# Seventy-two instead of sixty-seven seven-product pairs in the down projections of a two-layer encoder

## The chip, the core and the metric

The kernel runs on one core of one Trainium2 chip. A core has a matmul engine (TensorE, PE in the profile; its loading of stationary operands is PEld), an engine for element-wise work (VectorE, DVE), one that applies functions and copies (ScalarE, ACT), GpSimd (POOL) and SyncE (SP). Each issues its instructions in the order in which they were laid down and waits where an operand is not there yet. SP, ACT and POOL also issue transfers between the chip's memory and the core's. The metric is the device time of the whole kernel in microseconds, median over runs.

## The reference

Two encoder layers over one sequence of 256 tokens, width 2048, in float32. Each layer has an attention part with 12 heads of its own kind and 4 heads into 256 memory tokens, an output projection, and an MLP with a squared ReLU:

```
for i in range(2):
    h = rms_norm(x, norm_attn[i])
    ... heads = concat(token mixer's 12 heads, 4 memory heads)
    x = x + heads @ w_out[i]                        # 2048 x 2048
    h = rms_norm(x, norm_mlp[i])
    x = x + square(relu(h @ w_up[i])) @ w_down[i]   # 2048 x 8192, 8192 x 2048
```

Layer 0 has differential attention (two softmaxes subtracted), layer 1 windowed attention with a sink logit per head. The change bears on `@ w_down[i]`, the down projection of each layer, and on the first microseconds of the kernel.

## The kernel before

**Tiling.** Every weight matrix is cut into pieces of 128 x 1024 values (512 KB) and read once, in the order of one long list, the plan: input projection, memory projection, out, up and down of layer 0, then the same of layer 1. `fetch` takes the next piece from the plan: SP loads it into a raw tile (a `raw` buffer), and `split` makes two rounded halves of it, `hi` by a cast on ACT (line 443) and `lo`, the rest, by a subtraction on DVE (line 444). A product of float32 blocks is then three matmuls of 128x512 (x·hi, x·lo, and x's rest·hi), which `three` issues (lines 535 to 537; 496 to 498 in the input projection). `piece` keeps the fetched pieces two ahead of the matmuls.

**Down.** A down projection has two halves of the output columns, and each half goes through 32 k pairs. A k pair is two pieces. A **plain** pair takes eight products, 24 matmuls. A pair in the table of fast pairs takes **seven** products, 21 matmuls, with Winograd's scheme (function `seven`): it multiplies four sums of weight blocks (the tiles `a` and `b`, each 128x1024) and three differences of activation blocks (tile `t2`). For that DVE makes `b` in two additions of 128x512 (lines 357 and 358, in `sum_pair`), and `a` and `b` are each split into hi and lo: two casts more on ACT, two subtractions more on DVE. Tile `a` itself, piece one plus the upper part of piece two, was summed long before by transfers of POOL's queue into the chip's memory (`make_sums`, tensor `madesum`: a copy, then a transfer that adds), so that SP only loads it (line 339). These premade sums are spread over the plan by the steps in `SUM_GAP`. The differences of activations are made in the first half of down or in up, stored to memory (`kept`) and loaded by POOL for the half that uses them.

**Buffers.** The first piece of a fast pair, its `a` and its `b` lie in `slots`, a ring of six 128x1024 tiles (all named `big` in the profile). `load_pair` loads pairs up to three ahead (`LOOK`), as soon as a slot is free: the tile `a` of one fast pair goes into a slot that an earlier fast pair's first piece gives back when DVE has split it. The second piece's lower part goes into a 2 KB buffer (`t2k`). The split sums lie in tiles of the tags x2 or blk; in the second half of layer 0 the list `LATE_BLK` says which pair takes blk. They are returned when PE has used them.

**The order.** The program's text fixes the order on every engine: a scheduler lays each engine's instructions down once, and the wait queues are first in, first out. The tables `FAST` and `LATE` say which of the 32 pairs are fast. `FAST` (17 pairs) is used by both halves of layer 1 and the first half of layer 0, `LATE` (16) by the second half of layer 0:

```
WARM = 10
FAST = (2, 4, 6, 7, 9, 11, 12, 14, 16, 17, 19, 21, 22, 24, 26, 27, 29)
LATE = (2, 4, 6, 9, 11, 12, 14, 16, 17, 19, 21, 22, 24, 26, 27, 29)
LATE_BLK = (9, 12, 16, 19, 22, 26, 29)
```

**The start.** Ten matmuls of 128x128 on a tile `ones`, filled by DVE, run while the first transfers are under way (`WARM`, line 139). All x tiles and the first weight piece are loaded by SP. A tile `rw` holds a row of scalars, positions and sink logits, loaded once.

Of the kernel before, what the change touches and what calls it, by code (L numbers as in the profile page):

```python
# [14 lines left out]
F32 = mybir.dt.float32  # L15
F32R = mybir.dt.float32r
BF16 = mybir.dt.bfloat16
I32 = mybir.dt.int32
# [4 lines left out]
P = 128  # L23
S = 256
# [21 lines left out]
SQ_WAIT = 3  # L46
SINGLE = 4
AHEAD = 2
WARM = 10
FAST = (2, 4, 6, 7, 9, 11, 12, 14, 16, 17, 19, 21, 22, 24, 26, 27, 29)  # L50
LATE = (2, 4, 6, 9, 11, 12, 14, 16, 17, 19, 21, 22, 24, 26, 27, 29)
AWAY = range(6, 15)
LATE_BLK = (9, 12, 16, 19, 22, 26, 29)
LOOK = 3
KEEP_AFTER = (2, 6, 10, 14)
KEEP_LAST = (10, 18, 26, 34)
KEEP_GAP = 2
SUM_AT = {0: 44, 1: 2}
SUM_GAP = ({"in": 4, "mem": 4, "out": 4, "up": 11}, {"in": 4, "mem": 12, "out": 12, "up": 7})
LAM_INIT = 0.8 - 0.6 * math.exp(-0.3 * 0)  # L60

G_ATTN, G_MEM, G_MLP = 0, 2 * KT, 4 * KT
G_AQ, G_AK, G_BQ, G_BK = 96, 97, 98, 99
G_MQ, G_MK, G_SUB = 100, 102, 104
NG = 105
R_SINK = 256
R_POS = 268
NR = 524


@with_exitstack
def trunk(ctx: ExitStack, tc: tile.TileContext, xin, xtok, memin, memtok, posrel, gcol, rows,
          w_a, w_b, w_mem, w_out, w_up, w_down, out):
    nc = tc.nc

    cp = ctx.enter_context(tc.tile_pool(name="cp", bufs=1))
    wp = ctx.enter_context(tc.tile_pool(name="wp", bufs=4))
    xp = ctx.enter_context(tc.tile_pool(name="xp", bufs=1))
    tp = ctx.enter_context(tc.tile_pool(name="tp", bufs=1))
# [5 lines left out]
    def nm(s):  # L85
        uid[0] += 1
        return f"{s}{uid[0]}"

    def bank(tag="aux"):
        return pp.tile([P, 512], F32, tag=tag, name=nm(tag))  # L90
# [22 lines left out]
    def big(shape):  # L113
        return xp.tile(shape, F32, tag="big", name=nm("big"), bufs=1)

    def t2k(shape, dt=F32):
        return tp.tile(shape, dt, tag="t2k", name=nm("t2k"), bufs=7)

    def t1k():
        return tp.tile([P, 256], F32, tag="t1k", name=nm("t1k"), bufs=4)  # L120

    def small(n):
        return tp.tile([P, n], F32, tag="sm", name=nm("sm"), bufs=25)
# [4 lines left out]

    gc = cp.tile([P, NG], F32, name="gc")
    nc.scalar.dma_start(gc[:, 0:KT], gcol[:, 0:KT])  # L130
    xt = cp.tile([P, 2, D], F32, name="xt")
    nc.scalar.preload_act_table_set("natural_log_exp_and_others")
    ident = cp.tile([P, P], F32, name="ident")
    make_identity(nc, ident)
    ones = cp.tile([P, P], F32, name="ones")
    nc.vector.memset(ones, 1.0)
    warm = bank()
    for _ in range(WARM):
        nc.tensor.matmul(warm[:, 0:P], lhsT=ones, rhs=ones, start=True, stop=True)
    r2 = cp.tile([P, 2], F32, name="r2")  # L140
    ssq = cp.tile([P, 2, 4], F32, name="ssq")
    gs = cp.tile([P, 5], F32, name="gs")
    neglam = cp.tile([P, 1], F32, name="neglam")
    rw = cp.tile([P, NR], F32, name="rw")

    def inv_sqrt(dst, src, n):
        y = small(n)
# [92 lines left out]
    def fast_pairs(name, h):  # L240

        if name.startswith("out"):
            return OUT_FAST[h]
        if name.startswith("up"):
            return UP_FAST[h]
        if name.startswith("down"):
            return LATE if (name, h) == ("down0", 1) else FAST
        return ()

    def plan_pairs(name, n, halves=2):  # L250
# [25 lines left out]
    def sums_tag(key):  # L276
        if key[0].startswith("up"):
            return "h2"
        if key[0] == "down0" and key[1] == 1:
            return "blk" if key[2] in LATE_BLK else "x2"  # L280
        return "blk" if key[0].startswith("out") else "x2"
# [4 lines left out]
    def make_sums(layer):  # L286
# [15 lines left out]
        def step(i):  # L302
            if i:
                add(*wanted[i - 1])
            if i < len(wanted):
                copy(*wanted[i])
# [4 lines left out]
        for i in range(len(wanted) + 1):  # L311
            making.append((at, lambda i=i: step(i)))
            at += SUM_GAP[layer][max((k for k in SUM_GAP[layer] if at_piece[k, layer] <= at), key=lambda k: at_piece[k, layer])]

# [313 lines left out]
    def val_split(ps, st):  # L628
        hi = blk([P, 2, 512], F32R)
        lo = blk([P, 2, 512], F32R)  # L630
        for t in range(2):
            split_gain(hi[:, t, :], lo[:, t, :], ps[t], st[:, 2 + t:3 + t])
        return hi, lo
# [146 lines left out]
    tabs = {}  # L780

    def bias_distance():
        pr = cp.tile([P, 50], F32, name="posrel")
        with tc.issue_after(behind[0].ins):
            nc.sync.dma_start(pr, posrel)
        tabs["pr"] = pr
        pk, pq = pr[:, 0:2].bitcast(I32), rw[:, R_POS:R_POS + S].bitcast(I32)
        tabs["d"] = t2k([P, 2, S], I32)
        for t in range(2):
            nc.gpsimd.tensor_tensor(tabs["d"][:, t, :], pk[:, t:t + 1].broadcast_to([P, S]), pq, op=ALU.subtract)  # L790
# [70 lines left out]

    def load_rows():
        with tc.issue_after(behind[0].ins):
            nc.sync.dma_start(rw, rows.broadcast_to([P, NR]))
            nc.sync.dma_start(gc[:, KT:NG], gcol[:, KT:NG])

    def scalars():
        lv = rw[:, 0:256].rearrange("p (a b d) -> p a b d", a=2, b=2)
        pr = t1k()[:, 0:128].rearrange("p (a d) -> p a d", a=2)
        nc.vector.tensor_tensor(pr, lv[:, :, 0, :], lv[:, :, 1, :], op=ALU.mult)  # L870
        lm = small(2)
        nc.vector.tensor_reduce(lm, pr, axis=AX.X, op=ALU.add)
        le = small(2)
        nc.scalar.activation(le, lm, AF.Exp)
        nc.vector.tensor_tensor(neglam, le[:, 1:2], le[:, 0:1], op=ALU.subtract)
        nc.vector.tensor_scalar_add(neglam, neglam, -LAM_INIT)
        nc.vector.tensor_scalar_mul(gs[:, 0:1], gc[:, G_AQ:G_AQ + 1], 64 ** -0.5)
        nc.vector.tensor_scalar_mul(gs[:, 1:2], gc[:, G_BQ:G_BQ + 1], 128 ** -0.5)
        nc.vector.tensor_scalar_mul(gs[:, 2:4], gc[:, G_MQ:G_MQ + 2], 128 ** -0.5)
        nc.vector.tensor_scalar_mul(gs[:, 4:5], gc[:, G_SUB:G_SUB + 1], 1.0 - LAM_INIT)  # L880
# [64 lines left out]
    done_heads = {}  # L945
# [230 lines left out]
    X2 = Halves()  # L1176
    st0 = cp.tile([P, 4], F32, name="st0")

    xs = {}

    def load_x(k, n):
        if k % 4 == 0:
            xs[k // 4] = xp.tile([P, 4, S], F32, tag="h2", name=nm("xs"), bufs=6)
        nc.sync.dma_start(xs[k // 4][:, k % 4:k % 4 + n, :], xin[:, S * k:S * (k + n)].rearrange("p (k s) -> p k s", s=S))
# [13 lines left out]
    bias = big([P, 12, 2, S])  # L1198
# [5 lines left out]
    H2 = Halves(lambda pair: "h2" if pair < 6 else "x2")  # L1204
    make_sums(0)
    loads = Task([lambda c=c: load_residual(c) for c in range(4)], wait=RES_AT, gap=RES_GAP, front=True)
    for g in range(3):
# [18 lines left out]
        qT, qd = norm_T(ps, st0, 8, gs[:, 0:1])  # L1226
        ps = chunk_tok("a", 3 + g, X2)
        kT, kd = norm_T(ps, st0, 8, gc[:, G_AK:G_AK + 1])
# [3 lines left out]
    qm, qd = norm_T(ps, st0, 4, gs[:, 2:3])  # L1232
# [6 lines left out]
    H2 = Halves(lambda pair: "h2" if pair < 6 else "x2")  # L1239
    bias = bias_load()  # L1240
# [3 lines left out]
    kT, kd = norm_T(ps, st1, 4, gc[:, G_BK:G_BK + 1])  # L1244
    ps = chunk_tok("b", 4, X2)
    vv = val_split(ps, st1)
    for g in range(3):
        ps = chunk_tok("b", g, X2)
        qT, qd = norm_T(ps, st1, 4, gs[:, 1:2])
        for h in range(4):  # L1250
            n = 4 * g + h
            done_heads[n] = Task(plain_head(h, n // 3, qT, kT, vv, bias, rw[:, R_SINK + n:R_SINK + n + 1], H2, n), [qd, kd])
    ps = chunk_tok("b", 5, X2, mem_ahead)
    qm, qd = norm_T(ps, st1, 4, gs[:, 3:4])
    mem_part(1, qm, qd, H2)
# [71 lines left out]
```

## Time and profile before

| what | value |
|---|---|
| runs | 2071.48, 2071.71, 2073.93 us; median 2071.71 |
| profiled execution | 2070.87 us; its span 2069.1 us |
| matmuls busy (PE) | 2063.2 us, 9987 records |
| DVE, ACT, POOL busy | 1792.3, 1283.8, 179.9 us |
| down of layer 0, first half | 767 to 930 us |
| down of layer 0, second half | 930 to 1092 us |
| down of layer 1, first half | 1744 to 1906 us |
| down of layer 1, second half | 1906 to 2066 us |

The profile is of one execution, 0.84 us below the median of the runs. Busy time of PE counts pipelined matmuls whose ends are modelled: a 128x512 matmul is shown with 0.39 us although the next one starts 0.23 us later, so a matmul's cost is the distance of starts. The same holds, less strongly, for DVE and ACT. The rows by which the prediction argues stand there.

### The profile page before, as it was taken

What the parts mean: (1) busy time and instruction counts of PE and PEld (TensorE: products, weight loads), DVE (VectorE), ACT (ScalarE), POOL (GpSimd) and SP (SyncE); (2) the same over time, 40 slices, a digit from 0 to 9 for tenths busy, and PEclk for the clock granted to TensorE, in tenths of its full rate; (3) what the DMA queues carried; (4) which work ended last, traced back from release to release, by engine and by line L of the source; (5) the groups of instructions that cost most, each with busy time, mean ns of one, the idle gap of its engine ahead of it and who ended that gap; (6) DMA issues with size and microseconds to landing.
All of it is one profiled execution on the core that took longest, in us unless ns stands there. A gap on an engine that the chain in (4) does not pass through costs nothing.

```text
span 2069.1 us, 28771 instructions
## 1 busy us (share of the span) xinstructions
PE 2063.2 (100%) x9987; PEld 1715.1 (83%) x9987; DVE 1792.3 (87%) x2595; ACT 1283.8 (62%) x1912; POOL 179.9 (9%) x276
## 2 busy tenths in 40 slices
PE   9999999999999999999999999999999999999999
PEld 7888888888888888888888888888888888888887
DVE  7677777898998999998896677889998999999998
ACT  7467665556555577667665566556566566666764
POOL 1200111100010000000001110000001110000000
PEclk9999999999999999999999999999999999999999
DMA  9678997877888889988979887568889998998994
GB/s 316 243 241 271 278 289 226 275 231 224 267 283 280 289 280 337 363 290 281 343 277 298 270 261 214 193 217 253 255 269 315 307 300 301 341 356 309 299 361 167
DMA packets 172418, 577.80 MB, mean 279 GB/s; under 512 B 19936, under 2 KB 20960, under 8 KB 170976
## 3 DMA queue, kind: packets, MB, share of 16 engines
q1 hardware_dynamic: 133408, 441.19, 59.8%
q0 software_dynamic: 33824, 116.93, 22.0%
q10 hardware_dynamic: 5040, 17.84, 2.1%
q8 instruction: 78, 1.28, 0.2%
q14 instruction: 68, 0.56, 0.1%
HBM read 543.25 MB, written 100.79 MB: 311 GB/s over the span
## 4 chain that ended last, share of the span: by engine, by line
PE 97%; DVE 2%; DMA 1%; issue 0%; ACT 0%; SPq 0%; ACTq 0%; DVEq 0%
PE mm L536 12%; PE mm L537 12%; PE mm L535 12%; PE aux L536 11%; PE aux L537 11%; PE aux L535 11%; PE mm L496 7%; PE mm L497 7%; PE mm L498 7%; DVE lo L444 1%; PE aux L639 1%; PE mm L1043 1%; PE aux L1043 1%; PE aux L616 1%; PE aux L658 1%; PE aux L696 1%
## 5 line engine op out<-in xcount | busy, mean ns | idle before, releaser
L443 ACT CAST hi<-raw 128x1024 fp32r<-128x1024 f32 (+1 forms) x506 | 509.6, 1036 | 355.4 <-PE mm L498 109.4
L444 DVE TENSOR_TENSOR lo<-raw,hi 128x1024 fp32r<-128x1024 f32 (+1 forms) x506 | 600.5, 1203 | 148.8 <-ACT hi L443 147.4
L496 PE MATMUL mm<-hi,x 128*128 128x512 f32 x640 | 256.1, 402 | 0.5 <-ACT hi L443 0.5
L497 PE MATMUL mm<-lo,x 128*128 128x512 f32 x640 | 250.7, 392 | 0.2 <-DVE lo L444 0.2
L498 PE MATMUL mm<-hi,x 128*128 128x512 f32 x640 | 250.1, 391 | 0.0
L443 ACT CAST h<-big 128x1024 fp32r<-128x1024 f32 (+1 forms) x100 | 100.4, 1021 | 127.9 <-DVE big L284 83.6
L443 ACT CAST hi<-big 128x1024 fp32r<-128x1024 f32 (+1 forms) x149 | 132.4, 913 | 71.5 <-PE aux L537 35.8
L535 PE MATMUL mm<-hi,h 128*128 128x512 f32 (+1 forms) x441 | 171.1, 388 | 0.0
L536 PE MATMUL mm<-lo,h 128*128 128x512 f32 (+1 forms) x441 | 170.8, 387 | 0.0
L537 PE MATMUL mm<-hi,h 128*128 128x512 f32 (+1 forms) x441 | 170.8, 387 | 0.0
L536 PE MATMUL aux<-lo,h 128*128 128x512 f32 x422 | 164.6, 390 | 0.7 <-DVE lo L444 0.7
L535 PE MATMUL aux<-hi,h 128*128 128x512 f32 x422 | 164.4, 390 | 0.0
L537 PE MATMUL aux<-hi,h 128*128 128x512 f32 x422 | 164.2, 389 | 0.0
L535 PE MATMUL mm<-hi,x 128*128 128x512 f32 x414 | 161.7, 391 | 0.0
L537 PE MATMUL mm<-hi,x 128*128 128x512 f32 x414 | 161.1, 389 | 0.0
L536 PE MATMUL mm<-lo,x 128*128 128x512 f32 x414 | 161.1, 389 | 0.0
L444 DVE TENSOR_TENSOR lo<-big,hi 128x1024 fp32r<-128x1024 f32 (+1 forms) x149 | 152.8, 1045 | 3.2 <-ACT hi L443 3.2
L535 PE MATMUL aux<-hi,x 128*128 128x512 f32 x398 | 155.5, 391 | 0.0
L537 PE MATMUL aux<-hi,x 128*128 128x512 f32 x398 | 154.9, 389 | 0.0
L536 PE MATMUL aux<-lo,x 128*128 128x512 f32 x398 | 154.9, 389 | 0.0
L498 PEld LDWEIGHTS mm<-hi,x 128*128 128x128 f32 x640 | 120.2, 188 | 26.0
L444 DVE TENSOR_TENSOR h<-big,h 128x1024 fp32r<-128x1024 f32 (+1 forms) x100 | 116.4, 1179 | 28.7 <-ACT h L443 26.4
(309 smaller groups left out, 4285.3 us busy)
## 6 DMA issues: line engine op xcount, KB each, us to landing
raw<-in_w_up SPq DMA_DIRECT2D x164, 512.0 KB, 5.9
madesum<-in_w_down POOLq DMA_DIRECT2D x130, 512.0 KB, 6.7
raw<-in_w_down SPq DMA_DIRECT2D x122, 512.0 KB, 5.6
big<-in_w_up SPq DMA_DIRECT2D x92, 512.0 KB, 4.7
raw<-in_w_a SPq DMA_DIRECT2D x72, 512.0 KB, 5.1
h<-kept POOLq DMA_DIRECT2D x67, 512.0 KB, 5.7
big<-in_w_down SPq DMA_DIRECT2D x57, 512.0 KB, 5.4
big<-madesum SPq DMA_DIRECT2D x55, 512.0 KB, 5.3
```

What stands on the lines that cost most here:

```text
L443: nc.scalar.copy(hi, src)
L444: return nc.vector.tensor_tensor(lo, src, as32(hi), op=ALU.subtract)
L496: nc.tensor.matmul(ps[t], lhsT=xh, rhs=hi[:, ws], start=(k == 0), stop=False)
L497: nc.tensor.matmul(ps[t], lhsT=xh, rhs=lo[:, ws], start=False, stop=False)
L498: nc.tensor.matmul(ps[t], lhsT=xl, rhs=hi[:, ws], start=False, stop=(k == KT - 1))
L535: nc.tensor.matmul(acc_, lhsT=x(0), rhs=w2[0][:, ws], start=first_, stop=False)
L536: nc.tensor.matmul(acc_, lhsT=x(0), rhs=w2[1][:, ws], start=False, stop=False)
L537: nc.tensor.matmul(acc_, lhsT=x(1), rhs=w2[0][:, ws], start=False, stop=last_)
L616: nc.tensor.transpose(out=pt[:, h * P:(h + 1) * P], in_=qn[t][:, h * P:(h + 1) * P], identity=ident)
L639: nc.tensor.transpose(out=pt[:, kt * S + qt * P:kt * S + (qt + 1) * P], in_=p_of(qt)[:, kt * P:(kt + 1) * P], identity=ident)
L658: nc.tensor.matmul(ps[c][:, qt * S:(qt + 1) * S], lhsT=qT[a][r, hl, qs], rhs=kT[b][r, hl, :], start=(a + b == 0), stop=(a == 1))
L1043: nc.tensor.transpose(out=pt[:, oo * S + t * P:oo * S + (t + 1) * P], in_=u[n][t][:, o * P:(o + 1) * P], identity=ident)
```

## The change

- The tables: `LATE` now has 19 pairs and is used in the second half of down in both layers; `FAST`, for the first halves, is `LATE` without 11 and 20, 17 pairs as before but in other places. That makes 72 instead of 67 fast pairs, three more in layer 0's second half and two more in layer 1's. Past the first, they come as two fast pairs and one plain pair by turns.
- `LATE_BLK` is every second pair of `LATE` from its third on. `SUM_GAP`'s steps are shortened in two stages (70 instead of 65 premade sums).
- Two more activation differences per layer are made and kept in up, by the new tables.
- The warm-up block has nine matmuls instead of ten, on the tile `ident` (made by POOL), and the tile `ones` with its fill on DVE is gone.
- The first x tile is loaded by ScalarE's queue, ahead of everything but one small transfer there, and no longer by SP's.
- The row tile `rw` is a 2 KB buffer now instead of a tile of its own, with the 12 sink logits in a tile and a transfer of their own; there are eight 2 KB buffers instead of seven.

```diff
-WARM = 10
-FAST = (2, 4, 6, 7, 9, 11, 12, 14, 16, 17, 19, 21, 22, 24, 26, 27, 29)
-LATE = (2, 4, 6, 9, 11, 12, 14, 16, 17, 19, 21, 22, 24, 26, 27, 29)
+WARM = 9
+LATE = (2, 4, 5, 7, 8, 10, 11, 13, 14, 16, 17, 19, 20, 22, 23, 25, 26, 28, 29)
+FAST = tuple(j for j in LATE if j not in (11, 20))
-LATE_BLK = (9, 12, 16, 19, 22, 26, 29)
+LATE_BLK = LATE[2::2]
-SUM_GAP = ({"in": 4, "mem": 4, "out": 4, "up": 11}, {"in": 4, "mem": 12, "out": 12, "up": 7})
+SUM_GAP = ({"in": 4, "mem": 4, "out": 4, "up": 9}, {"in": 4, "mem": 8, "out": 10, "up": 7})
...
     def t2k(shape, dt=F32):
-        return tp.tile(shape, dt, tag="t2k", name=nm("t2k"), bufs=7)
+        return tp.tile(shape, dt, tag="t2k", name=nm("t2k"), bufs=8)
...
     nc.scalar.dma_start(gc[:, 0:KT], gcol[:, 0:KT])
+    xs = {0: xp.tile([P, 4, S], F32, tag="h2", name="xs0", bufs=6)}
+    nc.scalar.dma_start(xs[0][:, 0, :], xin[:, 0:S])
...
-    ones = cp.tile([P, P], F32, name="ones")
-    nc.vector.memset(ones, 1.0)
     warm = bank()
     for _ in range(WARM):
-        nc.tensor.matmul(warm[:, 0:P], lhsT=ones, rhs=ones, start=True, stop=True)
+        nc.tensor.matmul(warm[:, 0:P], lhsT=ident, rhs=ident, start=True, stop=True)
...
-    rw = cp.tile([P, NR], F32, name="rw")
+    sink = cp.tile([P, 12], F32, name="sink")
...
         if name.startswith("down"):
-            return LATE if (name, h) == ("down0", 1) else FAST
+            return LATE if h else FAST
...
-            nc.sync.dma_start(rw, rows.broadcast_to([P, NR]))
+            tabs["rw"] = t2k([P, NR])
+            nc.sync.dma_start(tabs["rw"], rows[:, 0:NR].broadcast_to([P, NR]))
+            nc.sync.dma_start(sink, rows[:, NR:NR + 12].broadcast_to([P, 12]))
...
     def load_x(k, n):
+        if k == 0:
+            return
```

In the rows that follow, each line is one instruction of an engine in its order: source line, operation, output, operands, size. Line numbers after the change are one lower than before from the warm-up on.

**PE at the kernel's start.** `ones` and `ident` are the warm-up's operands, `mm` the accumulators of the first input projection, `x` the first x tile and `hi`, `lo` the first weight piece, whose two halves are split one after the other. Before:

```order
L139 MATMUL aux_83<-ones 128x128 x10
L496 MATMUL mm_104<-hi_107,x_111 128x512
L496 MATMUL mm_105<-hi_107,x_111 128x512
L497 MATMUL mm_104<-lo_108,x_111 128x512
L498 MATMUL mm_104<-hi_107,x_111 128x512
```

With the change:

```order
L495 MATMUL mm_103<-hi_106,x_108 128x512
L496 MATMUL mm_103<-lo_107,x_108 128x512
L497 MATMUL mm_103<-hi_106,x_108 128x512
L495 MATMUL mm_104<-hi_106,x_108 128x512
L496 MATMUL mm_104<-lo_107,x_108 128x512
L497 MATMUL mm_104<-hi_106,x_108 128x512
L495 MATMUL mm_103<-hi_106,x_108 128x512
L496 MATMUL mm_103<-lo_107,x_108 128x512
L497 MATMUL mm_103<-hi_106,x_108 128x512
L138 MATMUL aux_83<-ident 128x128 x9
L495 MATMUL mm_104<-hi_106,x_108 128x512
```

The warm-up block stood ahead of the first real matmul; it now stands behind the ninth.

**ACT in the second half of layer 0's down.** `big` are the slots, `raw` the plain pieces, `hi` the pieces' casts, `blk` and `x2` the casts of the sums a and b, `h2` activations. Before, from the plain pair 25 to the fast pairs 26 and 27 (`blk2252` is the cast of 27's a, `hi2247` that of the first piece of 26):

```order
L443 CAST hi2238_10446<-raw2237_10445 128x1024
L443 CAST hi2245_10463<-raw2244_10462 128x1024
L443 CAST hi2247_10489<-big979_4686 128x1024
L443 CAST hi2256_10510<-t2k2220_10360 128x512
L443 CAST x22262_10548<-blk1648_7796 128x1024
L443 CAST h22266_10558<-t2k2249_10491 128x512
L443 CAST h22273_10594<-t2k2261_10544 128x512
L443 CAST blk2252_10497<-big979_4686 128x1024
L443 CAST hi2258_10538<-big979_4686 128x1024
```

With the change, from the plain pair 24 to the fast pairs 25 and 26 (`x22259` is the cast of 25's a, `hi2256` that of the first piece of 25, `blk2271` that of 26's a):

```order
L442 CAST hi2247_10449<-raw2246_10448 128x1024
L442 CAST hi2254_10466<-raw2253_10465 128x1024
L442 CAST x22259_10498<-big979_4685 128x1024
L442 CAST h22263_10508<-t2k2250_10456 128x512
L442 CAST blk2271_10551<-big979_4685 128x1024
L442 CAST hi2256_10492<-big979_4685 128x1024
L442 CAST x22261_10500<-blk1655_7815 128x1024
```

The cast of the second fast pair's a (`blk`) stood four places behind the first fast pair's `hi` before; now it stands one place ahead of it.

**DVE at the same place with the change**, from the lo part of the first piece of pair 25 to that of pair 26:

```order
L443 TENSOR_TENSOR lo2257_10493<-big979_4685,hi2256_10492 128x1024
L443 TENSOR_TENSOR x22262_10501<-blk1655_7815,x22261_10500 128x1024
L443 TENSOR_TENSOR lo2266_10514<-t2k2237_10404,hi2265_10513 128x512
L356 TENSOR_TENSOR big979_4685<-big979_4685 128x512
L443 TENSOR_TENSOR blk2272_10552<-big979_4685,blk2271_10551 128x1024
L357 TENSOR_TENSOR big979_4685<-big979_4685,t2k2249_10454 128x512
L443 TENSOR_TENSOR h22275_10561<-t2k2258_10494,h22275_10561 128x512
L443 TENSOR_TENSOR h22283_10601<-t2k2270_10547,h22283_10601 128x512
L443 TENSOR_TENSOR blk2274_10554<-big979_4685,blk2273_10553 128x1024
L443 TENSOR_TENSOR lo2268_10542<-big979_4685,hi2267_10541 128x1024
```

`lo2268` frees the slot of its pair's first piece, into which SP then loads the tile a of the pair two fast pairs further on (26's a, read by `blk2271`, lies where the first piece of 23 was). All ten stood so close together before only where two fast pairs follow each other; now they follow each other in every three pairs: five operations of 128x1024 and five of 128x512.

More of the change, by code (lines that the diff above doesn't have):

```diff
@@ L65 @@
 NG = 105
-R_SINK = 256
-R_POS = 268
-NR = 524
+R_POS = 256
+NR = 512
 @with_exitstack
@@ L786, in bias_distance @@
         tabs["pr"] = pr
-        pk, pq = pr[:, 0:2].bitcast(I32), rw[:, R_POS:R_POS + S].bitcast(I32)
+        pk, pq = pr[:, 0:2].bitcast(I32), tabs["rw"][:, R_POS:R_POS + S].bitcast(I32)
         tabs["d"] = t2k([P, 2, S], I32)
@@ L863, in load_rows @@
         with tc.issue_after(behind[0].ins):
-            nc.sync.dma_start(rw, rows.broadcast_to([P, NR]))
+            tabs["rw"] = t2k([P, NR])
+            nc.sync.dma_start(tabs["rw"], rows[:, 0:NR].broadcast_to([P, NR]))
+            nc.sync.dma_start(sink, rows[:, NR:NR + 12].broadcast_to([P, 12]))
             nc.sync.dma_start(gc[:, KT:NG], gcol[:, KT:NG])
     def scalars():
-        lv = rw[:, 0:256].rearrange("p (a b d) -> p a b d", a=2, b=2)
+        lv = tabs.pop("rw")[:, 0:256].rearrange("p (a b d) -> p a b d", a=2, b=2)
         pr = t1k()[:, 0:128].rearrange("p (a d) -> p a d", a=2)
@@ L1177, in trunk @@
     st0 = cp.tile([P, 4], F32, name="st0")
-    xs = {}
     def load_x(k, n):
+        if k == 0:
+            return
         if k % 4 == 0:
@@ L1251, in trunk @@
             n = 4 * g + h
-            done_heads[n] = Task(plain_head(h, n // 3, qT, kT, vv, bias, rw[:, R_SINK + n:R_SINK + n + 1], H2, n), [qd, kd])
+            done_heads[n] = Task(plain_head(h, n // 3, qT, kT, vv, bias, sink[:, n:n + 1], H2, n), [qd, kd])
     ps = chunk_tok("b", 5, X2, mem_ahead)
@@ L1298 @@
         rel[g::4, 12 * g:12 * g + 12] = a["rel_bias"]
-    rows = np.concatenate([a["a_lambda_q1"], a["a_lambda_k1"], a["a_lambda_q2"], a["a_lambda_k2"], a["b_sink"], pos.reshape(1, S).view(np.float32)], axis=1)
+    rows = np.concatenate([a["a_lambda_q1"], a["a_lambda_k1"], a["a_lambda_q2"], a["a_lambda_k2"], pos.reshape(1, S).view(np.float32), a["b_sink"]], axis=1)
     arrays = {
```

## The prediction

> **What bounds the kernel now.** I read the page's busy times first, then its chain, then what PE waited for, then the four halves of the down projections as windows.
>
> ```profile
> span 2069.1 us, 28771 instructions
> PE 2063.2 (100%) x9987; PEld 1715.1 (83%) x9987; DVE 1792.3 (87%) x2595; ACT 1283.8 (62%) x1912; POOL 179.9 (9%) x276
> PE 97%; DVE 2%; DMA 1%; issue 0%; ACT 0%; SPq 0%; ACTq 0%; DVEq 0%
> ```
>
> PE is busy for 2063.2 of 2069.1 us, and 97% of the chain is its matmuls. What is taken from PE's program comes off the time, so long as everything else still arrives ahead of it. The waits of PE over the whole run:
>
> ```profile
> PE aux L139 <- DVE ones L136: 1.1, 1, 1.1
> PE aux L536 <- DVE lo L444: 0.7, 2, 0.5
> PE mm L496 <- ACT hi L443: 0.5, 2, 0.3
> PE mm L497 <- DVE lo L444: 0.2, 1, 0.2
> ```
>
> All but the second row are in the first 10 us. That second row, PE waiting for a `lo` from DVE, comes from a down projection. Columns of the windows: length, then PE, PEld, DVE, ACT and POOL busy, granted clock, DMA share, GB/s.
>
> ```profile
> 767.00:930.00 163.00, 163.00 (x729) 135.24 (x728) 154.19 (x184) 113.93 (x148) 10.62 (x20) 1.00 0.93 331
> 930.00:1092.00 162.00, 161.27 (x716) 132.59 (x715) 144.20 (x172) 103.99 (x131) 11.17 (x17) 1.00 0.85 301
> 1744.00:1906.00 162.00, 162.00 (x725) 134.38 (x724) 153.75 (x183) 112.32 (x141) 10.63 (x20) 1.00 0.95 336
> 1906.00:2066.00 160.00, 159.77 (x717) 132.59 (x715) 144.80 (x172) 100.32 (x122) 7.92 (x15) 1.00 0.81 285
> ```
>
> Only layer 0's second half shows PE short of its window, by 0.73 us. DVE has the least room beside PE: 17.8 us idle in that half, 15.2 in layer 1's second half, about 8 in the first halves, where PE is full all the same.
>
> **The matmuls taken away.** A fast pair issues 21 matmuls where a plain one issues 24. Ten matmuls in a row give the price by their starts:
>
> ```profile
> 764.82 0.39 PE L537 MATMUL mm<-hi,h 128*128 128x512 f32 x1
> ...
> 766.86 0.39 PE L537 MATMUL mm<-hi,h 128*128 128x512 f32 x1
> ```
>
> 2.04 us over nine steps is 0.2267 each. Five more fast pairs save 5 x 3 = 15 matmuls, **−3.40 us**. A plain pair takes PE 24 x 0.2267 = 5.44, a fast one 4.76, and the new rhythm of two fast and one plain 14.96 us.
>
> **The warm-up block.** At the start:
>
> ```profile
> 1.05 3.88 PE L139 MATMUL aux<-ones 128*128 128x128 f32 x20 [1.05 <-DVE ones L136]
> 5.13 0.73 PE L496 MATMUL mm<-hi,x 128*128 128x512 f32 x2 [0.19 <-ACT hi L443]
> ...
> 8.10 0.50 PE L497 MATMUL mm<-lo,x 128*128 128x512 f32 x1 [0.23 <-DVE lo L444]
> ...
> 9.36 0.39 PE L496 MATMUL mm<-hi,x 128*128 128x512 f32 x1
> ```
>
> Each warm-up instruction leaves two records, 20 in 3.88 us, 0.194 apiece; the real matmuls start at 5.13, and the first tile's twelve are issued when the thirteenth starts at 9.36. The block costs nothing now: it fills the wait for the first weights. In the new order it stands between the ninth and the tenth matmul, so its 18 records run while the next operands are there or nearly there.
>
> ```profile
> 0.74 0.39 SPq L1184 DMA_DIRECT2D xs<-in_xin  x1
> 1.19 0.42 SPq L416 DMA_DIRECT2D raw<-in_w_a  x1
> 4.46 0.62 ACT L443 CAST hi<-raw 128x512 fp32r<-128x512 f32 x1 [0.69 <-DMA raw<-in_w_a]
> 6.70 0.63 ACT hi L443
> 7.35 0.70 DVE lo L444
> 767.25 1.75 PE aux L1043 x16
> ```
>
> With the x load off SP's queue the weight transfers are issued 0.45 us earlier (1.19 to 0.74), and its casts at 4.46 and 6.70 move as much. The first `hi` is then ready at 4.63, its `lo` (0.70) about 5.4, the second `lo` at 8.05 − 0.45 = 7.6. At full clock the ninth matmul would end about 8.1. Sixteen transposes of the same size and type take 1.75 us, 0.109 each, so 18 records take 1.96, three matmuls 0.68: the twelve are done at 10.7, against 9.36 **+1.4**. But the first matmuls are then also the first work of PE, and the warm-up's own records show what that costs: 0.194 beside 0.109, a ratio of 1.78, though the window's clock column reads 1.00 everywhere. Nine cold matmuls at 0.404 and a warm block behind them give about 11.3, **+1.9**; all of it cold, 3.5 us for the block and 0.40 for each of the last three, 13.3, **+3.9**. Below, the bound is +0.3: the block fits partly into the wait for the second `lo`, should the transfer come later than now. I take **+1.7**, between the first two, because the rows show the slow rate for 3.9 us and nothing later. PE never catches this up, as it is full behind it.
>
> The Trainium skill, "TensorE: Matmul & The Clock Gate", Part 1, says that PE runs at half clock until about 3.4 us of sustained work have passed, in a window that does not start with the kernel; the trace agrees in that the 18 extra-slow records last about that long. By it the sum would have +1.9 here, and up to +3.9 where the window lies badly, instead of +1.7.
>
> **The sums in layer 0's second half.** A fast pair asks more of DVE. Its prices by starts, and the lead over PE:
>
> ```profile
> 1010.29 0.69 DVE L358 TENSOR_TENSOR big<-big,t2k 128x512 f32<-128x512 f32 x1
> 1010.89 0.68 DVE L444 TENSOR_TENSOR h<-t2k,h 128x512 fp32r<-128x512 f32 x1
> 1011.49 1.22 DVE L444 TENSOR_TENSOR lo<-big,hi 128x1024 fp32r<-128x1024 f32 x1
> 1012.63 1.22 DVE L444 TENSOR_TENSOR x<-big,x 128x1024 fp32r<-128x1024 f32 x1
> ...
> 1015.59 0.39 PE L536 MATMUL mm<-lo,h 128*128 128x512 f32 x1
> ```
>
> 0.60 us for 128x512, 1.14 for 128x1024. A converted pair adds two additions (1.20) and two wide splits (2.28) and saves half a split (0.54): +2.94. Three of them add 8.8 to 144.2, and the window shrinks by 2.0: idle falls from 17.8 to about 7 of 160. Two fast pairs and a plain one take DVE 14.5 of PE's 14.96. DVE still fits; but PE uses that `lo` (ended 12.71) at 15.59, a **lead of 2.9 us**, and now a loop runs through it. The tile a of the second fast pair goes into the slot that the lo of the fast pair two back has freed. In the new order of ACT its cast stands ahead of the first fast pair's `hi` cast, which ten DVE operations follow, the last of them the lo that frees the next slot. The trace has such a wait:
>
> ```profile
> 1019.58 1.22 DVE L444 TENSOR_TENSOR lo<-big,hi 128x1024 fp32r<-128x1024 f32 x1
> 1020.82 0.33 SPq L339 DMA_DIRECT2D big<-madesum  x1
> 1026.98 1.05 ACT L443 CAST blk<-big 128x1024 fp32r<-128x1024 f32 x1 [5.07 <-DMA big<-madesum]
> 1027.93 2.00 ACT L443 CAST hi<-raw 128x1024 fp32r<-128x1024 f32 x2
> ...
> DMA to landing us min/median/max: 3.5/5.2/6.7
> ```
>
> The lo ends at 1020.80, the load is issued at once, the cast starts 6.2 us later with ACT idle for 5.07. The last row is all of line 339's loads in this half: median 5.2. One turn of the loop: 5.2 + two casts of 0.95 (1026.98 to 1027.93) + ten operations (5 x 1.14 + 5 x 0.60 = 8.7) + 0.1 = 15.9 against 14.96: **1.0 us late per turn**. The order differs a little from turn to turn; worked out in the same way the nine turns lose 1.0, 0.6, 0.1, 0.5, 1.6, gain 0.75, and lose 0.4, 1.0, 1.3, together 5.7. The lead of 2.9 pays for the first part, the rest, **2.8 us**, falls on PE. Against it stands what PE waits there now:
>
> ```profile
> 954.38 0.40 PE L535 MATMUL aux<-hi,h 128*128 128x512 f32 x1
> 954.94 0.50 PE L536 MATMUL aux<-lo,h 128*128 128x512 f32 x1 [0.16 <-DVE lo L444]
> ...
> 1041.53 0.39 PE L535 MATMUL aux<-hi,h 128*128 128x512 f32 x1
> 1042.45 0.50 PE L536 MATMUL aux<-lo,h 128*128 128x512 f32 x1 [0.53 <-DVE lo L444]
> ```
>
> Starts 0.56 and 0.92 apart instead of 0.23 are 0.33 and 0.69 lost; with smaller delays beside them some 1.7 in this half. If the new rhythm replaces these, the net is **+1.1**. Bounds: −1.7, if all waits vanish (landing below about 4.8), and +8.3 with landing at 6.0, 0.8 more in each of nine turns.
>
> The Trainium skill, "DMA: Bandwidth & Descriptors", "Anatomy of one DMA", gives 2 us and the bytes at 436 GB/s for a transfer by GpSimd's queue: an estimate of 3.2 us for 512 KB. By that each turn would have 1 us to spare, no wait would be left and the net be −1.7. The trace's median for SP's loads in this half disagrees, and the measurement decides.
>
> **Layer 1's second half**: two more fast pairs, DVE idle from 15.2 to about 8 of 158.6. In this half the casts of a stand behind the `hi` casts in ACT's order, as in the first halves now; the same arithmetic leaves 3.4 us or more per turn. Cost 0; −0.2 (its window's gap now) to +5 if it starts to wait as layer 0 does. The first halves keep 17 pairs and get denser runs of six; two plain pairs behind each run give DVE 5.1 us back. Cost 0.
>
> **What hides the rest.**
>
> ```profile
> L546 DVE TENSOR_TENSOR t2k<-blk 128x256 f32<-128x256 f32 x16 | 6.6, 420 | 3.0 <-ACT blk L1046 2.9
> 624.00:676.00 52.00, 52.00 (x239) 43.32 (x238) 46.18 (x59) 28.96 (x37) 4.27 (x7) 1.00 0.84 285
> 707.44 1.09 POOL L296 DMA_DIRECT2D madesum<-in_w_down  x1 [6.76 <-DMA madesum<-in_w_down]
> ```
>
> Two kept differences more per layer cost DVE 0.42 and three smaller operations each, about 1.7, inside up, where DVE is idle 5.8 of 52 us; uncovered, 3 us. Three and two more premade sums go to POOL's queue, whose last addition of layer 0 is out at 707, 60 us before down; if that cover were gone, the first fast pairs would wait for it, one turn of the loop each. The sink's own small transfer on SP, and the eighth 2 KB buffer, lie under PE's full lead: 0.
>
> **Sum.** 2070.87 (the profiled execution) − 3.40 + 1.7 + 1.1 = 2070.3. The median of the runs is 0.84 above that execution, so **2071.1 us**. A measurement tells about 0.2% from no change, 4.1 us.
>
> **Rivals.**
> - **The slow start takes all twelve matmuls and the block** (+3.9 in place of +1.7): 2073.3, no change. For it the 0.194 of all twenty records; against it that nothing shows the slow rate beyond 3.9 us.
> - **The loop binds.** With a loads landing after 6.0 us instead of 5.2, since five premade tiles and their sums are added to 301 GB/s and the first halves already run at 331, every turn in layer 0's second half is 0.8 us worse: 9 x 0.8 = 7.2 on top, 2078.3, slower. From a landing of about 5.7 it is slower by more than 0.2%. For it: the maximum of 6.7 and the 5.07 idle; against it: at 331 GB/s PE waits for nothing, though there no cast of a stands ahead.
> - **The block and the waits cost nothing**: −3.4 + 0.3 − 1.7 = −4.8, 2066.9, faster. For it that the transfers' minimum is 3.5; against it two things have to hold at once.
> - **DVE's idle time cannot shrink**, as it is made of waits for buffers that PE returns: the 17.8 and 15.2 us stay instead of falling to 7 and 8, and the halves get 18 us longer: 2089, slower. Against it the first halves, which run with 8.
>
> **Chances**: the sum as forecast, or within 2068 to 2075, 0.52; slow start 0.14; loop 0.16; nothing costs 0.12; DVE 0.06. Faster 0.12, same 0.66, slower 0.22. The range, 2067.0 to 2078.5, reaches from the best case to the loop's and leaves out DVE's and half of what lies at the ends.
>
> **What would show it.** PE's matmul records fewer by 15 and the warm-up; the warm-up's row between 7 and 13 us instead of at 1.05, and the thirteenth matmul about 11.1; in layer 0's second half PE's waits on `lo` of about 2.8 us, with ACT idle for `madesum` ahead of `blk` casts in most turns; none in layer 1. A PE wait on a `lo` in layer 1's second half, or on `kept` or `hid` anywhere, would make the forecast wrong, and so would a mean landing off 5.2 by half a microsecond.

## The result: slower by 0.4%, and the profile after

| | before | changed |
|---|---|---|
| median of the runs | 2071.71 us (5 runs, 2070.47 to 2073.93) | 2081.52 us (5 runs, 2078.65 to 2083.54) |
| ratio to before, 95% interval | | 1.0044 (1.0033 to 1.0055) |
| profiled execution, its span | 2070.87, 2069.1 us | 2082.12, 2080.3 us |

The forecast was no change, 2071.1 us, with a range to 2078.5. The change costs 9.8 us between the medians, and 11.3 us between the two profiled executions, which the stages below account for. The page of the changed kernel, busy times and chain:

```profile
span 2080.3 us, 28841 instructions
PE 2062.0 (99%) x9970; PEld 1711.8 (82%) x9970; DVE 1809.6 (87%) x2630; ACT 1291.3 (62%) x1926; POOL 189.7 (9%) x291
PE 91%; DMA 4%; DVE 4%; issue 1%; ACT 1%; ACTq 0%; DVEq 0%
```

PE's own work did get less (before 2063.2 us and 9987 records; the 17 that are missing are 15 matmuls and two of the warm-up), but the chain, 97% PE before, now passes through transfers and DVE for 8% of the span. What PE waited for:

```profile
PE mm L535 <- DVE lo L443: 5.5, 7, 1.0
PE mm L495 <- ACT x L438: 5.4, 1, 5.4
PE aux L535 <- DVE lo L443: 1.5, 2, 0.8
PE aux L769 <- DVE t2k L443: 1.3, 1, 1.3
PE aux L476 <- DVE xt L1108: 0.6, 2, 0.3
```

Nine waits for a `lo` (7.0 us) where the down projections had two (0.7), and one wait in layer 1's attention (line 769). Seven of the nine are in layer 0's second half, one in each first half. To place the loss I compared the starts of the same matmuls in the two profiled executions. The difference, read at a place at the end of each stage (a landmark, below), gives by subtraction what the stage cost:

| stage | matmuls saved | stage longer by |
|---|---|---|
| start, to 45 us | | +2.16 |
| 45 to 765 us | | +0.16 |
| layer 0, down, first half | | +1.06 |
| layer 0, down, second half, and the passage to layer 1 | 9 (−2.04) | +6.31 |
| layer 1, attention and what follows, to 1740 us | | +1.88 |
| layer 1, down, first half | | +1.14 |
| layer 1, down, second half | 6 (−1.36) | −1.36 |
| sum | 15 (−3.40) | +11.35 |

Layer 0's second half lost 6.3 us although it had 2.04 us less to do: its waits grew by 8.35. Of the 6.31, 4.92 are there when layer 1's first matmuls start, and 1.39 come right behind them, where PE's transposes (line 476) wait for DVE, which is late. The windows (same columns as in the prediction) for the halves in order:

```profile
770.00:934.00 164.00, 163.24 (x727) 135.11 (x725) 155.53 (x187) 113.70 (x148) 10.10 (x19) 1.00 0.91 324
934.00:1102.00 168.00, 162.17 (x713) 131.42 (x712) 152.38 (x182) 107.15 (x138) 12.53 (x20) 1.00 0.86 303
1756.00:1917.00 161.00, 160.15 (x714) 132.55 (x713) 153.59 (x185) 112.04 (x142) 10.09 (x19) 1.00 0.93 330
1917.00:2078.00 161.00, 160.12 (x718) 132.89 (x716) 152.74 (x180) 103.45 (x127) 8.97 (x17) 1.00 0.83 297
```

PE is short of its window by 5.8 us in layer 0's second half, by 0.8 in each first half. In layer 1's second half the whole gain arrived; its 0.9 lie at the end of the kernel.

**The loop in layer 0's second half.** ACT, DVE and SP there, one turn of it:

```profile
999.87 0.33 SPq L338 DMA_DIRECT2D big<-madesum  x1
...
1006.53 1.05 ACT L442 CAST blk<-big 128x1024 fp32r<-128x1024 f32 x1 [4.04 <-DMA big<-madesum]
1007.49 1.04 ACT L442 CAST hi<-big 128x1024 fp32r<-128x1024 f32 x1
...
1008.56 1.23 DVE L443 TENSOR_TENSOR lo<-big,hi 128x1024 fp32r<-128x1024 f32 x1 [2.37 <-ACT hi L442]
...
1016.73 1.22 DVE L443 TENSOR_TENSOR lo<-big,hi 128x1024 fp32r<-128x1024 f32 x1
...
1017.98 0.33 SPq L338 DMA_DIRECT2D big<-madesum  x1
```

It is the loop that the prediction described (before the change the cast of a stood five places behind the `hi` cast): a load of a is issued when a `lo` has freed its slot, ACT idles for 4.04 us ahead of the cast, with the `hi` cast behind it, DVE idles for 2.37 us, and the `lo` that ends at 1017.95 lets the next load go. This turn took 18.1 us (999.87 to 1017.98), where PE needs 14.96: 6.6 for the load to land, 2.0 for the two casts and 9.4 for DVE, which ran without a pause from the first `lo` to the second. The longest pieces of the chain that start between 984 and 1070 us are the loop's loads themselves (start, us):

```profile
984.25 5.29 DMA blk<-madesum
999.87 6.64 DMA big<-madesum
1034.29 7.30 DMA blk<-madesum
1051.84 6.96 DMA big<-madesum
1069.67 4.53 DMA big<-madesum
```

With the one issued at 1017.98 the turns were 15.6, 18.1, 16.3, 17.6 and 17.8 us, 85.4 in all against 5 x 14.96 = 74.8: 10.6 late, of which the lead paid 2 to 3 and PE the rest. The five loads took 33.4 us to land instead of 5 x 5.2 = 26.0; the rest of the five turns, 52.0 us, is no longer than the prediction's 5 x 10.7 = 53.5. The chain also names loads of hidden tiles (`t2k<-hid`, up to 4.29 us in these turns), but DVE did not pause for them on the loop.

### The profile page after: what moved, and what is told of

Its sections match the earlier page's. It is cut to its first block, busy times and chain, and to the rows that moved or that the text cites. A ratio compares the mean times of both kernels' runs of the same rounds, so it can differ in the third digit from the quotient of the medians.

```text
span 2080.3 us, 28841 instructions
## 1 busy us (share of the span) xinstructions
PE 2062.0 (99%) x9970; PEld 1711.8 (82%) x9970; DVE 1809.6 (87%) x2630; ACT 1291.3 (62%) x1926; POOL 189.7 (9%) x291
## 4 chain that ended last, share of the span: by engine, by line
PE 91%; DMA 4%; DVE 4%; issue 1%; ACT 1%; ACTq 0%; DVEq 0%
PE mm L535 11%; PE mm L536 11%; PE mm L534 11%; PE aux L535 10%; PE aux L536 10%; PE aux L534 10%; PE mm L495 7%; PE mm L496 7%; PE mm L497 7%; DVE lo L443 2%; DMA big<-madesum 1%; DMA t2k<-hid 1%; PE aux L1044 1%; PE mm L1044 1%; PE aux L638 1%
## 5 line engine op out<-in xcount | busy, mean ns | idle before, releaser
L443 DVE TENSOR_TENSOR lo<-raw,hi 128x1024 fp32r<-128x1024 f32 (+1 forms) x496 | 588.0, 1203 | 129.6 <-ACT hi L442 128.6
L442 ACT CAST hi<-raw 128x1024 fp32r<-128x1024 f32 (+1 forms) x496 | 499.9, 1036 | 308.7 <-PE mm L497 120.4
L535 PE MATMUL aux<-lo,h 128*128 128x512 f32 x392 | 152.8, 390 | 1.5 <-DVE lo L443 1.5
L534 PE MATMUL aux<-hi,h 128*128 128x512 f32 x392 | 152.8, 390 | 0.0
L536 PE MATMUL aux<-hi,h 128*128 128x512 f32 x392 | 152.6, 389 | 0.0
```

The source lines that it names most:

```text
L442: nc.scalar.copy(hi, src)
L443: return nc.vector.tensor_tensor(lo, src, as32(hi), op=ALU.subtract)
L534: nc.tensor.matmul(acc_, lhsT=x(0), rhs=w2[0][:, ws], start=first_, stop=False)
L535: nc.tensor.matmul(acc_, lhsT=x(0), rhs=w2[1][:, ws], start=False, stop=False)
L536: nc.tensor.matmul(acc_, lhsT=x(1), rhs=w2[0][:, ws], start=False, stop=last_)
```

## The experiments

Each run's stage lengths were read as in the table above. Diffs are against the changed kernel where nothing else is said.

### The old start

```diff
+    ones = cp.tile([P, P], F32, name="ones")
+    nc.vector.memset(ones, 1.0)
-WARM = 9        # on ident
+WARM = 10       # on ones
-    nc.scalar.dma_start(xs[0][:, 0, :], xin[:, 0:S])
```

> The changed kernel with the old start alone: the warm-up of ten matmuls on the tile that DVE fills, ahead of the first real matmul, and the first x tile on SP's queue. In the trace of the change the thirteenth matmul starts 2.7 us later than before and a landmark at 43 us 2.16 us later. Theory (the start costs PE time that never comes back): 2.2 us less than the changed kernel's 2081.5, about 2079.3, with the landmark back at +0.0. Rival (PE waits for later data anyway, so the delay is absorbed in the second half of layer 0's down): no less than 2081.0.

2077.37 us (10 runs), ratio to before 1.0025 (1.0016 to 1.0034); against the changed kernel 4.2 us less. The landmark at 45 us is back at +0.27, which settles the start itself. The rest of the gain came in layer 0's second half (+3.4 instead of +6.3) and in layer 1's attention (+0.6 instead of +1.9). The changed kernel's five executions scatter by 5 us (2078.65 to 2083.54), and why those two stages changed here is not shown, so only the start is read from this run. The rival, absorption, is out.

The two halves of that edit, each alone and with one execution each:

```diff
 x on ScalarE's queue kept, old warm-up:
+WARM = 10, on ones, ahead of the first matmul
```

> The changed kernel with the old warm-up (ten matmuls on the tile that DVE fills, laid down ahead of the first real matmul) and the first x tile still on ScalarE's queue. Theory (what is lost at the start is the slow clock and the block in line): the landmark at 43 us comes back from +2.2 to about +0.3, the rest being the first matmul at 5.40 instead of 5.13. Rival (the x tile's later arrival holds everything): it stays above +1.5.

```diff
 new warm-up kept:
-    nc.scalar.dma_start(xs[0][:, 0, :], xin[:, 0:S])
+    nc.sync.dma_start(...)     # in load_x, as before
```

> The changed kernel with its new warm-up block and the first x tile on SP's queue as before. Theory: the nine slow matmuls and the block in line stay, so the landmark at 43 us stays at +1.7 or more. Rival (the queue of the x tile is the loss): it falls below +0.7.

With the old warm-up 2078.22 us and the landmark at −0.30; with the x tile back on SP 2080.97 us and the landmark at +1.42, less than the 1.7 expected but far above the rival's 0.7. The rows say why. The changed kernel's start:

```profile
5.40 0.80 PE L495 MATMUL mm<-hi,x 128*128 128x512 f32 x1 [5.40 <-ACT x L438]
6.00 0.63 PE L496 MATMUL mm<-lo,x 128*128 128x512 f32 x1
6.42 0.63 PE L497 MATMUL mm<-hi,x 128*128 128x512 f32 x1
...
9.38 2.17 PE L138 MATMUL aux<-ident 128*128 128x128 f32 x18
11.30 0.48 PE L495 MATMUL mm<-hi,x 128*128 128x512 f32 x1
...
12.09 0.40 PE L495 MATMUL mm<-hi,x 128*128 128x512 f32 x1
```

Nine matmuls, from the second on 0.42 to 0.43 us apart, then the block in 1.92 us (9.38 to 11.30; 0.107 a record, where the old block took 0.194), then 0.23 apart: the thirteenth starts at 12.09 instead of 9.36. The granted clock reads 1.00 in these microseconds too; that PE was slow is read from the distances of the starts. With the old warm-up and x on ScalarE's queue:

```profile
1.06 4.63 PE L140 MATMUL aux<-ones 128*128 128x128 f32 x20 [1.06 <-DVE ones L137]
5.50 0.60 PE L497 MATMUL mm<-hi,x 128*128 128x512 f32 x1
5.94 0.39 PE L498 MATMUL mm<-lo,x 128*128 128x512 f32 x1
6.17 0.40 PE L499 MATMUL mm<-hi,x 128*128 128x512 f32 x1
```

The first matmul is as late (5.50), yet from the second on they come 0.23 apart, and nothing is lost. So the loss is the slow first matmuls and the block in line. With the x tile back on SP and the new warm-up the slow stretch is there again, from an earlier first matmul:

```profile
4.79 0.80 PE L494 MATMUL mm<-hi,x 128*128 128x512 f32 x1 [4.79 <-ACT hi L441]
...
7.81 0.54 PE L494 MATMUL mm<-hi,x 128*128 128x512 f32 x1
8.19 0.39 PE L495 MATMUL mm<-lo,x 128*128 128x512 f32 x1
```

The x tile, issued behind another transfer on ScalarE's queue at 1.19 us, delays the first matmul (5.40 against 4.79 with x on SP). Whether that costs time is not shown: the landmarks differ by 0.7 us (2.16 and 1.42), but in six executions with the changed start (this kernel and five of the forms below) the landmark lies between +1.66 and +3.11, and in five with the old start between −0.45 and +0.68.

### The old pairs in layer 0's second half

```diff
-            return LATE if h else FAST
+            return (LATE_B if (name, h) == ("down0", 1) else LATE) if h else FAST
+LATE_B = (2, 4, 6, 9, 11, 12, 14, 16, 17, 19, 21, 22, 24, 26, 27, 29)
+LATE_BLK = (9, 12, 16, 19, 22, 26, 29)
```

> The changed kernel with the old sixteen pairs and their old buffer list in the second half of layer 0's down alone. There the change lost 6.3 us by the landmarks though it saves 2.0 us of matmuls, so waits grew by 8.3. Theory (the rhythm of two fast and one plain pair closes the loop lo - load of a - cast - lo): the half is back at its old length, 6.3 us less, about 2075.2. Rival (the loss comes from what the change adds elsewhere, more traffic and POOL's additions, and would be there with any list): at most 2 us less, 2079.5 or more.

2081.23 us (5 runs), no gain. The half itself, passage included, was back: longer than before by 0.1 instead of 6.3 us. But the old sixteen pairs are no subset of the others as the new ones are: together with the first half's seventeen they make 24 different pairs, so 24 differences of activations must be made, stored and loaded instead of 19. The stretch from 420 to 765 us, mostly up, got 3.9 us longer and the first half 3.4. The edit was no clean test; for the half it agrees with the loop. That the added differences made the other losses is likely, but not shown.

### ACT's order

```diff
+                    first_cast[name, c] = nc.scalar.copy(hi, raw)      # split's cast, remembered
 ...
-        split(ah, al, a)
+        with tc.issue_after(first_cast[name, c].ins):      # second half of layer 0's down only
+            split(ah, al, a)
```

> The changed kernel, all 72 pairs, with one condition on ACT's order in the second half of layer 0's down: the cast of a pair's tile a is laid down behind the hi cast of the fast pair ahead of it, never before it. Theory (ACT's place of that cast makes the loop): its turn gets shorter by a cast and five of the DVE operations, about 6 us, so it has 3 us or more to spare, and the waits of 8.3 us fall under 3: 2076 or less. Rival (DVE at 152 of 168 us and the transfers' landing are the limit, not the order): the waits stay above 6, 2079.5 or more.

2071.65 us (10 runs), ratio to before 0.9999 (0.9990 to 1.0009): 9.9 us less than the changed kernel, with the same pairs, bytes and buffers. Layer 0's second half is now 3.82 us shorter than before, the 2.04 of the matmuls and the 1.78 that PE waited there before. ACT at the place where the loop was:

```profile
1017.80 1.05 ACT L407 CAST hi<-big 128x1024 fp32r<-128x1024 f32 x1 [0.55 <-PE aux L542]
...
1020.48 1.06 ACT L448 CAST blk<-big 128x1024 fp32r<-128x1024 f32 x1 [1.11 <-DMA big<-madesum]
```

The cast of a still waits for its load (1.11 us), but the `hi` cast has gone ahead. Windows of 975 to 1075 us, the changed kernel's and this one's:

```profile
975.00:1075.00 100.00, 94.59 (x407) 75.54 (x407) 89.38 (x105) 62.42 (x79) 6.33 (x12) 1.00 0.92 323
```

```profile
975.00:1075.00 100.00, 100.00 (x443) 82.81 (x442) 99.56 (x118) 70.74 (x88) 6.33 (x12) 1.00 0.90 326
```

At the same traffic, DVE is busy for 99.6 of 100 us and PE for all of them. Neither DVE's load nor the rate of the transfers was the limit: the order was. The passage to layer 1 lost nothing here either, so its 1.39 us belonged to the loop.

### Seven 2 KB buffers

```diff
-        return tp.tile(shape, dt, tag="t2k", name=nm("t2k"), bufs=8)
+        return tp.tile(shape, dt, tag="t2k", name=nm("t2k"), bufs=7)
```

> The changed kernel with seven 2 KB buffers instead of eight. Theory (the eighth buffer is needed: four of the loop's turns pass through a load of a hidden tile into such a buffer): layer 0's second half gets longer by 1 to 4 us; and if the 1.9 us lost in layer 1's attention come from the order that the eighth buffer led to, they vanish: 2080 to 2084 in all. Rival (the buffer does nothing in down): the half's length within 0.7 us of the changed kernel's.

2083.79 us (4 runs), ratio 1.0052 (1.0037 to 1.0067). Layer 0's second half is 6.2 us longer than before, as with eight: the buffer does nothing there. The first halves lose more (2.9 and 2.0 us instead of 1.1 each), and the loss in layer 1's attention is almost gone (0.15), though this run lost 1.1 us more in layer 1's up, where the changed kernel lost nothing.

### A seventh slot

```diff
-        wide = big([P, 6, 4, S])
+        wide = big([P, 7, 4, S])
-        slots.extend(wide[:, i] for i in range(5))
+        slots.extend(wide[:, i] for i in range(6))
-    ... tag="t2k", bufs=8
+    ... tag="t2k", bufs=6      # pays for it
```

> The changed kernel with a seventh slot for the pieces and sums of fast pairs, paid for by two of the eight 2 KB buffers; ACT's order there still has casts of a ahead of earlier work. Theory (the loop goes through the slot): with one more slot a load of a no longer waits for the lo just made, so layer 0's second half shrinks by 4 us or more against the changed kernel's, though the 2 KB buffers are fewer. Rival (only ACT's order matters, or the 2 KB buffers): no gain there, or a loss.

In this run the added slot lay on the tile with the last chunk's hidden activations, which changes the products of pairs 30 and 31; its 2071.36 us are not used. A second form keeps that tile apart (`wide[:, 6]`):

> As the run with the seventh slot before, with the last chunk's hidden activations in a tile of their own, so that the seventh slot is a real one (six 2 KB buffers instead of eight pay for it). Theory (the loop goes through the slot): layer 0's second half shorter than the changed kernel's by 4 us or more. Rival (the gain of the other run came from the tile that two uses shared): within 1 us of the changed kernel's.

2072.68 us (one execution), and layer 0's second half 3.80 us shorter than before: the whole gain again, without a word on ACT's order and with two 2 KB buffers less. Line 338's loads between 975 and 1075 us and who waited for them, the changed kernel's first:

```profile
  ACT blk L442: 22.1, 6
...
DMA to landing us min/median/max: 3.5/5.3/7.3
```

With the seventh slot:

```profile
  ACT blk L442: 0.4, 1
...
DMA to landing us min/median/max: 4.0/5.4/7.7
```

The transfers landed no sooner, but their issue no longer waited for the `lo` just made, and ACT waited 0.4 us instead of 22.1. Two edits that share nothing but the loop, one breaking it at ACT's order and one at the slot, give the same 3.8 us.

### Both repairs together, and the kept differences

```diff
 old start, and the order of casts as above
```

> Both together in the changed kernel with its 72 pairs: the old start, and the cast of a laid down behind the hi cast ahead of it in the second half of layer 0's down. Theory (the two losses are separate and add up): 2071.65 with the order alone, less 1.8 at the start and about 1.4 in layer 1's attention, where the old start gave 0.6 instead of 2.0: 2068.4, faster than before by about 0.17%. Rival (the waits return once PE is earlier at the loop, as its loads then have less time): the second half of layer 0 is longer than with the order alone by 1 us or more, 2070 or more.

2069.33 us (11 runs), ratio 0.9990 (0.9981 to 1.0000). The second half kept its 3.82, so the rival (waits return) is out; the sum is 0.9 above the forecast, since the first half of layer 0 lost 1.9 here. The chain of the changed kernel shows what happens in that half:

```profile
794.63 0.61 DVE h L443
...
795.26 6.12 DMA kept<-h
...
801.41 0.03 ACT h L442
...
801.93 1.05 ACT x L442
...
807.63 0.69 DVE lo L443
...
808.36 0.50 PE mm L535
```

A difference is stored (6.12 us), its buffer comes back, only then can ACT cast the next hidden tile `h` into it, and behind that cast stand the casts of a fast pair. The last chunk of up hands over its four hidden tiles in down's first microseconds, and of their pairs, 28 to 31, 28 and 29 are fast now, where only 29 was. So:

```diff
-KEEP_LAST = (10, 18, 26, 34)
+KEEP_LAST = (2, 18, 26, 34)      # 28's difference earlier
```

> The version with the old start and the order of casts, with the difference for pair 28 made right behind its hidden tile (a wait of 2 steps instead of 10). In the first half of each down PE waits about 1 us for a lo behind an h cast that a store of a kept difference holds up (6.1 us to land). Theory (that store, one more in down's first pairs than before): the first half of layer 0 loses 0.3 instead of 1.9 us, that of layer 1 nothing: 2067.5 to 2068. Rival (the wait comes from the denser run of pairs): no change, 2069.3.

```diff
-KEEP_LAST = (10, 18, 26, 34)
+KEEP_LAST = (22, 30, 26, 34)     # 28's and 29's later
```

> The same version with the differences for pairs 28 and 29 made later in down (22 and 30 steps instead of 10 and 18), past the first run of fast pairs. Theory (the store holds an h buffer at the wrong moment): the wait in the first halves moves or goes, 2067.5 to 2069. Rival (the denser run): 2069.3, the wait at its old place.

2067.91 (ratio 0.9980, 0.9970 to 0.9989) and 2067.72 us (0.9976, 0.9967 to 0.9986), 10 runs each. The first halves lose 0.36 and 0.34 us in the early form, 0.30 and 0.0 in the late, so the store and not the denser run made the wait. Both beat the kernel before, by 0.2%, and the changed one. What PE still waits for in the late form:

```profile
PE aux L776 <- DVE t2k L450: 1.4, 1, 1.4
PE aux L139 <- DVE ones L136: 1.1, 1, 1.1
PE mm L502 <- ACT hi L449: 0.4, 1, 0.4
PE mm L503 <- DVE lo L450: 0.2, 1, 0.2
```

Nothing of the down projections is left in it. The first row is layer 1's attention, 1.7 us by the landmarks. Seven buffers had been without it, so:

```diff
 the late form, with
-    ... tag="t2k", bufs=8
+    ... tag="t2k", bufs=7
```

> The version with late keeps, with seven 2 KB buffers instead of eight. With eight it loses 1.7 us in layer 1's attention, where PE waits 1.4 us for a split of probabilities; the changed kernel loses 1.9 there, with seven buffers 0.15. Theory (the order that the eighth buffer leads to makes that wait, and down does not need the buffer): the attention's loss goes, nothing comes back elsewhere, about 2066.2. Rival (down's first halves need the eighth buffer, where seven cost 1.8 us in layer 0 and 0.8 in layer 1): 2068 or more.

2069.70 us (10 runs), ratio 0.9989 (0.9979 to 0.9999). The attention's wait stayed (1.2 us of PE's waits, 1.4 by the landmarks), and the first halves lost 1.2 and 1.1. The theory fell; the eighth buffer is worth about 2 us in the first halves of this form.

## Why the prediction was wrong, step by step

- **The matmuls taken away, −3.40: right.** PE issued 15 matmuls fewer, and with the loop broken the gain arrived in both second halves (−2.04 in −3.82, and −1.36).
- **The warm-up block, +1.7: mechanism right, the size within the scatter.** 2.16 us at the landmark, 1.66 to 3.11 in the six executions with this start. Of the two sums that the prediction stood between, the one with nine slow matmuls came: PE's first matmuls ran 0.427 apart, the block behind them 0.107 a record. The thirteenth matmul started at 12.09, 1.0 later than the 11.1 forecast: the x tile is later on ScalarE's queue, so that the first matmul came at 5.40, where the sum of 11.3 implies 5.0, and the slow matmuls took 0.427 instead of 0.404. Against "PE never catches this up", 0.6 us of the 2.7 came back before 45 us. The rival with all twelve slow (+3.9) did not come. (The old block that the prediction reads as 18 slow records has 20, in 3.88 us.) The Trainium skill, "TensorE: Matmul & The Clock Gate", section "Wait — 56ns, not 53.3ns?", gives 426.7 ns between the starts of cold matmuls of 512 columns; the trace agrees, 0.427. The same page's rule of about 3.4 us until full clock, in its section "What's actually happening", is near as well: 4.0 us here (5.40 to 9.38), and 3.0 to 3.4 with x on SP (from 4.79 to between 7.81 and 8.19).
- **The sums in layer 0's second half, +1.1: the step that failed.** Its loop was the right one, with the right lines and the sign. What it mis-sized was the landing in one turn: 5.2, the median of all of line 339's loads before the change. With the change the sixteen loads of that line still have a mean of 5.2 and a median of 4.9, but the five that the turns waited for took 5.3, 6.6, 7.2, 7.3 and 7.0 us, 6.7 on average, and the others 3.5 to 5.9. That is 7.4 us more in five turns, and waits grew by 8.35 us instead of 1.1. Why those loads were slow stays open. Four of them, of 6.6 to 7.3, were issued while four or five other transfers of SP were under way; but so was one of 5.3, and before the change two loads with only two others under way took 6.5 and 6.8. The rival "the loop binds" had named 8.3 for this term, with a chance of 0.16; the loop was its mechanism, but that the size agrees is in part luck, since it counted nine turns 0.8 us worse each and the trace has five, 1.5 worse each.
- **The Trainium skill's estimate of 3.2 us** for a transfer of this size ("DMA: Bandwidth & Descriptors", "Anatomy of one DMA"), which is made for GpSimd's queue and from which no wait would follow, did not hold for SP's loads, as the prediction said: no load of a in this half landed under 3.46 us, and those on the loop took up to 7.3.
- **Layer 1's second half, 0: right.** With the casts of a behind the `hi` casts there, the full 1.36 us came, although line 338's loads took 4.3 to 7.5 us there, with a median of 5.8, longer than in layer 0: here, where no loop runs through them, the slower landings cost nothing. That the same pairs cost 6.3 us in one layer and gained 1.4 in the other is the best sign in the profile that their number was not the cause.
- **"The first halves ... Cost 0" and "Two kept differences more ... inside up": wrong by 2.2 us.** The count was right, but one of the two (pair 28's) is made by the last chunk's schedule, in the first pairs of down. I had looked at DVE's slack and at the slots, and not at the buffer that a store holds for 6 us.
- **Layer 1's attention, +1.9: not seen at all.** PE's line 769 waits 1.3 us for a split of probabilities on DVE. Before the change and then with it:

```profile
1256.34 1.72 ACT L439 ACTIVATE x<-h,gc 128x256 fp32r<-128x256 f32 x4 [0.61 <-DMA h<-in_memin]
...
1279.45 1.23 DVE L444 TENSOR_TENSOR lo<-raw,hi 128x1024 fp32r<-128x1024 f32 x1 [0.18 <-ACT hi L443]
1280.59 0.68 DVE L444 TENSOR_TENSOR t2k<-aux,t2k 128x512 fp32r<-128x512 f32 x1
```

```profile
1269.47 1.71 ACT L438 ACTIVATE x<-h,gc 128x256 fp32r<-128x256 f32 x4 [4.05 <-DMA h<-in_memin]
...
1290.77 1.21 DVE L443 TENSOR_TENSOR lo<-raw,hi 128x1024 fp32r<-128x1024 f32 x1
1291.90 1.28 DVE L443 TENSOR_TENSOR t2k<-aux,t2k 128x512 fp32r<-128x512 f32 x2
```

  The split stands behind the same `lo` in both, and DVE's order is the same in the 50 us before; DVE is late. The last load of memory tokens (`h<-in_memin`) is issued 2.0 us later, measured against PE's matmuls, and lands 3.4 us later; ACT waits 4.05 us for it instead of 0.61, and DVE for ACT. In all runs with the change this load is issued 1.6 to 2.3 us later, and the loss goes with its landing: where it lands up to 2.0 us later the attention loses 0 to 0.15 (seven or six buffers in the changed kernel), at 2.4 to 2.7 it loses 0.6 to 0.8, at 3.3 to 3.7 1.4 to 2.1 (among them seven buffers in the late form). Why it comes late is open; the load before it already took 9.9 us instead of 7.8, although it was issued at the same place.
- **The sum.** 2.3 up to 765 us, 1.06 and 1.14 in the first halves, 6.31, 1.88 and −1.36 make the 11.35; the prediction had −0.6. Of the difference of 12, the loop is 7.3, the first halves 2.2, the attention 1.9 and the start 0.5.

## What to carry to other kernels

Where a loop runs through a buffer, a transfer and an engine's queue, price its transfer by the loads that lie on the loop, at the worst row seen, not by the line's median; a loop forecast 1 us late per turn was 2.1 us late here. Look first for the waiting instruction that stands ahead of work which needs nothing from it: laying these casts down later, with no other change, was worth 9.9 us here, more than all the matmuls that the change saved. And when an edit adds an operation to a table, find the time at which that table's schedule runs it, and which buffer its store holds.

## What the runs showed of the hardware that was not expected

- With 323 and 326 GB/s in the same 100 us, single 512 KB loads took from 3.5 to 7.3 us in the changed kernel and from 4.3 to 6.3 with the other order of ACT. The mean rate said nothing about the time of one load.
- DVE can run at 99.6% of a 100 us window beside a PE at 100%, with ACT at 71%, without PE waiting.
- With ten matmuls of 128x128 while the first load is under way, the real matmuls ran 0.23 us apart from the second on; with such a block behind the ninth real matmul, the first ones ran 0.43 apart and the block took 1.92 us of its own. Between these starts lie about 2 us of the kernel's time, on the average of six and five executions.
